# First MLP product: the first two products of seven pairs, instead of three, ahead of half 1 of h^T

## The chip, the core and the metric

One core of a Trainium2 chip runs the whole kernel. The time is device time in microseconds (us) for one execution, inputs and output in HBM; lower is better.

## What is computed

One encoder block on a sequence of 1024 positions with 1024 channels, all in float32. The part that matters here is its second half, the MLP:

```
x  = layer_norm(ALPHA * x + (1 + g1) * mix) * ln1_g + ln1_b      # mix: the mixer's output through w_out
h2 = layer_norm_plain(x) * (1 + sc2) + sh2
ff = square(relu(h2 @ w_ff1 + b_ff1)) @ w_ff2 + b_ff2             # 1024 -> 4096 -> 1024
return layer_norm(ALPHA * x + (1 + g2) * ff) * ln2_g + ln2_b
```

## The kernel before

All matrix products take each operand as the sum of a rounded part and a remainder (type fp32r), and make three matmuls of each product: high x high, high x low, low x high (`mm3`, lines 131 to 133). Rounding is a cast, usually on ScalarE; the remainder is a subtraction, on VectorE or GpSimd.

The first MLP product is h^T = h2 transposed (1024 channels, in 8 blocks `kt` of 128, by 1024 positions) against the 4096 columns of `w_ff1`. It runs as one level of a Strassen-Winograd scheme: positions are cut into two halves of 512, channels into two halves of four blocks, and the columns into 16 pairs (`NPR`) of two blocks of 128. A pair needs seven products instead of eight; each of them is 12 matmuls of 128x128 against 128x512 (4 blocks times three). Its seven right sides are B11 and B21 (half 0 of the positions, plain columns of h^T), B22, T1, T2, T3 and T4 (half 1, or sums and differences with half 1). Its left sides are the plain weight block `w1` (line 945, `w1_plain`), a quarter `w22`, and two blocks `ws` of sums of weights. The first two products of a pair, w1 against B11 and B21, need nothing of half 1.

Around it the order is this. For each half of the positions: the projection by `w_out` (`wo_pass`), the layer norm `ln1` for four tiles of 128 positions (its result `xn2`), and then the transposition into `h_col` (four 128x128 transposes into one PSUM bank of tag c, an ACTIVATE that scales them, line 932). For half 0 the columns are rounded on VectorE (line 967) with the remainder on GpSimd (line 968) and written to HBM (`hb_d`, line 969). For half 1 the T operands are built from them on VectorE: lines 1016, 1017, 1028, 1036 for the sums and `split_h` (936, 937) for rounding. While this goes on TensorE does the first two products of the first three pairs (`EARLY = 3`); their results stay in the six PSUM banks of tags a and b until their pairs come, in the loop over the pairs at the end. Program text: the weights of the early pairs are split ahead of half 1's layer norm, their products stand behind half 1's transposes and T operands.

In that loop, `ff1_products` makes the seven (or remaining five) products of a pair, evicts them with sums (`hidden`), and squares: three of the four results in one VectorE operation (`square`, line 1071), one with a Relu on ScalarE (1106) and a GpSimd multiplication (1107). `ff1_prep` loads the next pair's weights and makes its `ws` on GpSimd (1094 to 1097); `ff1_sums` makes three sums on GpSimd (1140 to 1143) and writes seven tiles of 128x512 to HBM (`hid_d`), from where the second MLP product reads them.

No order between the engines is written by hand in this part. Tiles are declared with a pool, a tag and a number of buffers, and all waits follow from them. The order on each engine and on each DMA queue is fixed when the program is built (`schedule_with_timeline_sim`): instructions are placed by a model of their times, with the program's order as their rank. `xp` holds three raw buffers, of which the gains and offsets of the layer norm (`lg`, `lb`) take two until it is done. Half 0's `xn2` tiles lie in the buffers `wh1` and `wl1`, `w1` in `wh0` and `wl0`. Pool `hp` begins where the layer norm's pools end, and pool `o8p` where those with half 1's `xn2` end.

Of the kernel before, what the change touches and what calls it, by code (L numbers as in the profile page):

```python
# [12 lines left out]
ALU = mybir.AluOpType  # L13
# [13 lines left out]

EARLY = 3

# [59 lines left out]
def body(ctx, tc, x, c, w_ada, b_ada, w_in, b_gate, norm_w, w_out, ln1_g, ln1_b,  # L89
# [20 lines left out]
    def bank(tag):  # L110
        return ps.tile([P, 512], F32, name="ps" + tag, tag=tag, bufs=NB[tag])
# [832 lines left out]

    def w1_plain(i, rv):
        w_ = gw1.tile([P, 2, KT, P], F32R, name="w1", tag=("wh0", "wl0")[i % 2], bufs=1)
# [4 lines left out]
    w1p = {}  # L951
# [22 lines left out]

    KH = KT // 2
    lo, hi = slice(0, KH), slice(KH, KT)
    t2 = [a1w.tile([P, KH, 512], F32R, name=f"t2{n_}", tag=f"w{n_}1", bufs=1) for n_ in "hl"]
# [4 lines left out]

    def s_sums(r0, r1, rs, eng):

        eng.tensor_add(out=rs[:, hi], in0=r1[:, lo], in1=r1[:, hi])
        eng.tensor_sub(out=rs[:, lo], in0=r0[:, lo], in1=r1[:, lo])
        eng.tensor_sub(out=r0[:, lo], in0=rs[:, hi], in1=r0[:, lo])
        eng.tensor_sub(out=r0[:, hi], in0=r0[:, hi], in1=r0[:, lo])
# [10 lines left out]
    def hp_raw(n_):  # L999
        return hp.tile([P, 1024], F32, name=n_, tag="pr", bufs=3)  # L1000

    r0, r1, rs = [hp_raw(n_).rearrange("p (k n) -> p k n", k=KT) for n_ in ("r0", "r1", "rs")]
    tbs = [hp.tile([P, 512], F32, name=f"tb{kt}") for kt in range(KH)]
# [5 lines left out]
    for kt in range(KH):  # L1009
        nc.sync.dma_start(out=hb[kt], in_=hb_d[kt * P:kt * P + P, :])  # L1010
    s_sums(r0, r1, rs, nc.vector)
    for kt in range(KH):
        h_col(hp, kt, xn2s, b12s[kt])
        h_col(hp, KH + kt, xn2s, b22s[kt])
    for kt in range(KH):
        nc.vector.tensor_sub(out=hb[kt], in0=b12s[kt], in1=hb[kt])
        nc.vector.tensor_sub(out=tbs[kt], in0=b22s[kt], in1=hb[kt])
        split_h(tbs[kt], t2[0][:, kt], t2[1][:, kt], nc.vector)
    a1es.close()
    o8es, o8p = pool("o8p", "left")  # L1020
# [23 lines left out]

    hq = lambda kt, lo, x_: hR[:, x_, kt, lo:lo + 512]
    B11 = lambda kt: (hq(kt, 0, 0), hq(kt, 0, 1))
    B21 = lambda kt: (hq(KH + kt, 0, 0), hq(KH + kt, 0, 1))
    B22 = lambda kt: (hq(KH + kt, 512, 0), hq(KH + kt, 512, 1))
# [4 lines left out]

    def prod(pb, a_, b_, first, last):
        for kt in range(KH):
            ks = slice(kt * P, kt * P + P)
            mm3(pb, a_[0][:, ks], a_[1][:, ks], *b_(kt), first and kt == 0, last and kt == KH - 1)

    def quarter(w_, q_):
        return [w_[:, x_].rearrange("p k n -> p (k n)")[:, q_ * 512:q_ * 512 + 512] for x_ in range(2)]  # L1060

    def tq(name, bufs):
        return tp.tile([P, 512], F32, name=name, tag=name, bufs=bufs)

    def hidden(pb, u_, bias):
        h_ = tq("hq", 8)
        nc.vector.scalar_tensor_tensor(out=h_, in0=pb, scalar=bias, in1=u_, op0=ALU.add, op1=ALU.add)
        return h_

    def square(h_):  # L1070
        nc.vector.scalar_tensor_tensor(out=h_, in0=h_, scalar=0.0, in1=h_, op0=ALU.max, op1=ALU.mult)  # L1071
        return h_

    def ff1_first(i):
        pa, pb = bank("a"), bank("b")
        prod(pa, quarter(w1p[i], 0), B11, True, True)
        prod(pb, quarter(w1p[i], 1), B21, True, True)
        return pa, pb

# [7 lines left out]

    def ff1_prep(i):
        r0, r1 = w1_raw(2 * i), w1_raw(2 * i + 1, tp)
        if i not in w1p:  # L1090
            w1p[i] = w1_plain(i, r0)
        w22 = split_22(r1[:, hi])

        nc.gpsimd.tensor_add(out=r1[:, hi], in0=r1[:, lo], in1=r1[:, hi])
        nc.gpsimd.tensor_sub(out=r1[:, lo], in0=r0[:, lo], in1=r1[:, lo])
        nc.gpsimd.tensor_sub(out=r0[:, lo], in0=r1[:, hi], in1=r0[:, lo])
        nc.gpsimd.tensor_sub(out=r0[:, hi], in0=r0[:, hi], in1=r0[:, lo])  # L1097
        return [w22] + split_s((r0, r1), (op8[2 * i % 3], op8[(2 * i + 1) % 3]))

    def ff1_products(i, w22, wa, wb):  # L1100
        ba, bb = bf1[:, 2 * i:2 * i + 1], bf1[:, 2 * i + 1:2 * i + 2]
        pa, pb = early.pop(i) if i in early else ff1_first(i)
        s1 = tq("s1", 2)
        nc.scalar.copy(out=s1, in_=pa)
# [18 lines left out]
        if i:  # L1123
            h21 = square(hidden(pb4, s1, bb))
        pb = bank("a" if i == 0 else "c")
        prod(pb, quarter(wb, 1), T1, True, True)
        h22 = hidden(pb, s1, bb)
# [4 lines left out]
        h12 = square(hidden(pb, u2, ba))  # L1132
        if not i:
            h21 = square(hidden(p4(), s1, bb))
        return h11, h21, h12, h22

    def ff1_sums(i, h11, h21, h12, h22):
# [12 lines left out]
    ops = [split_22(r22)] + ws0  # L1150
    for i in range(NPR):
# [191 lines left out]
```

## Time and profile before

| | |
|---|---|
| three runs | 1126.03, 1127.18, 1129.0 us; median 1127.18 |
| profiled execution | 1127.42 us, its span 1125.4 us |
| mean granted TensorE clock | 0.964 of 2.4 GHz |
| busy share of the span | TensorE 93%, VectorE 74%, ScalarE 36%, GpSimd 33% |
| HBM | 148.29 MB read, 44.05 MB written |

Times in the trace count from the span's start. PE is TensorE, DVE VectorE, ACT ScalarE, POOL GpSimd, SP the queue that issues most DMAs. A granted clock of 1.00 is 2.4 GHz, lower ones are means over stretches at 2.4 and 1.2 GHz. The end of a matmul is modelled, so that a dense stream is read from one start to the next. In the chain, `L131` is line 131, and the line can be that of a helper.

### The profile page before, as it was taken

Reading aid. Unit: us, or ns where it says so; the run is one execution under the profiler, and the core shown is the slowest. Engines: PE = TensorE matmul, PEld = TensorE weight load, DVE = VectorE, ACT = ScalarE, POOL = GpSimd, SP = SyncE. Lnnn points to the kernel's source line nnn. Section 1 sums busy time; section 2 is a strip of 40 time slices with the busy share of each in tenths; the row PEclk is TensorE's granted clock in tenths of the full one; section 3 lists DMA queues with packets and bytes.
Section 4 is the critical chain, followed back from the end, with each engine's and each line's share of the span. In section 5 each row is a group of like instructions: output and inputs, shape, how many; then the busy total and the mean of one; then the engine's idle time right before and its main releaser. Section 6 shows DMA issues by size and latency. Waiting matters only on the chain.

```text
span 1125.4 us, 14177 instructions
## 1 busy us (share of the span) xinstructions
PE 1047.7 (93%) x5033; PEld 854.1 (76%) x5033; DVE 836.1 (74%) x1479; ACT 401.1 (36%) x692; POOL 375.1 (33%) x271
## 2 busy tenths in 40 slices
PE   5899989899999898749999999999998999999995
PEld 3678988797777686538688888888876888888884
DVE  7944775867678499798786766575666797667997
ACT  3353225553455124552222312223243333333420
POOL 3554214634123022209788776765300000000000
PEclk8999989899899899969999999999998999999998
DMA  9916504433133713624545444535987886688502
GB/s 305 289 53 239 184 9 136 132 99 107 58 113 112 253 57 126 210 67 148 187 146 183 147 163 135 174 122 184 342 315 242 285 285 215 206 277 266 169 36 93
DMA packets 140566, 193.27 MB, mean 172 GB/s; under 512 B 9088, under 2 KB 70476, under 8 KB 140496
## 3 DMA queue, kind: packets, MB, share of 16 engines
q1 hardware_dynamic: 121808, 158.81, 42.7%
q10 hardware_dynamic: 18688, 33.56, 8.8%
q8 instruction: 39, 0.64, 0.2%
q14 instruction: 31, 0.25, 0.1%
HBM read 148.29 MB, written 44.05 MB: 171 GB/s over the span
## 4 chain that ended last, share of the span: by engine, by line
PE 45%; DVE 10%; DMA 3%; POOL 2%; issue 2%; ACT 1%; SPq 0%; ACTq 0%; DVEq 0%; POOLq 0%
PE psb L133 6%; PE psb L132 6%; PE psb L131 6%; PE psa L132 5%; PE psa L133 5%; PE psa L131 5%; PE psc L133 4%; PE psc L132 4%; PE psc L131 4%; DMA raw<-in_w_ff_dram 1%; DMA acc<-x_d 1%; DVE ln_st L150 1%; DVE o L1174 1%; DVE acc L1316 1%; DVE acc L914 1%
## 5 line engine op out<-in xcount | busy, mean ns | idle before, releaser
L1173 ACT CAST o<-hraw 128x1024 fp32r<-128x1024 f32 x56 | 58.6, 1050 | 141.9 <-PE psc L133 93.8
L1174 DVE TENSOR_TENSOR o<-hraw,o 128x1024 fp32r<-128x1024 f32 x56 | 71.7, 1284 | 40.9 <-ACT o L1173 40.8
L131 PE MATMUL psa<-wh,hR 128*128 128x256 f32 (+2 forms) x268 | 81.6, 305 | 0.5 <-DVE acc L890 0.5
L133 PE MATMUL psa<-wh,hR 128*128 128x256 f32 (+2 forms) x268 | 80.3, 300 | 0.0
L132 PE MATMUL psa<-wl,hR 128*128 128x256 f32 (+2 forms) x268 | 80.1, 299 | 0.0
L132 PE MATMUL psa<-o,o 128*128 128x512 f32 x176 | 69.4, 394 | 6.9 <-DVE o L1174 6.9
L133 PE MATMUL psa<-o,o 128*128 128x512 f32 x176 | 69.4, 394 | 0.0
L131 PE MATMUL psa<-o,o 128*128 128x512 f32 x176 | 69.0, 394 | 0.2 <-ACT o L1173 0.2
L994 ACT CAST ws<-raw 128x1024 fp32r<-128x1024 f32 x30 | 31.0, 1050 | 104.2 <-POOL raw L1097 94.3
L132 PE MATMUL psb<-o,o 128*128 128x512 f32 x160 | 63.0, 394 | 0.0
L133 PE MATMUL psb<-o,o 128*128 128x512 f32 x160 | 62.9, 393 | 0.0
L261 POOL TENSOR_TENSOR wl<-raw,wh 128x256 fp32r<-128x256 f32 (+2 forms) x27 | 37.9, 1425 | 73.6 <-ACT wh L260 73.6
L131 PE MATMUL psb<-o,o 128*128 128x512 f32 x160 | 62.4, 392 | 0.0
L1140 POOL TENSOR_TENSOR hq<-hq 128x512 f32<-128x512 f32 x16 | 34.5, 2157 | 63.5 <-DVE hq L1071 51.5
L131 PEld LDWEIGHTS psa<-wh,hR 128*128 128x128 f32 x268 | 53.2, 198 | 2.6 <-DVE acc L890 1.2
L132 PEld LDWEIGHTS psa<-wl,hR 128*128 128x128 f32 x268 | 53.1, 198 | 2.0 <-issue 0.9
L133 PEld LDWEIGHTS psa<-wh,hR 128*128 128x128 f32 x268 | 53.0, 198 | 1.1
L995 DVE TENSOR_TENSOR ws<-raw,ws 128x1024 fp32r<-128x1024 f32 x30 | 40.6, 1357 | 13.9 <-ACT ws L994 13.7
L1173 ACT CAST o<-raw 128x1024 fp32r<-128x1024 f32 x32 | 33.3, 1048 | 46.8 <-DVE raw L1216 16.2
L416 POOL TENSOR_TENSOR m<-m,mraw 128x512 f32<-128x512 f32 x28 | 39.7, 1416 | 30.8 <-ACT mraw L415 9.7
L1071 DVE SCALAR_TENSOR_TENSOR hq<-hq 128x512 f32<-128x512 f32 x48 | 49.4, 1031 | 0.6
L132 PEld LDWEIGHTS psa<-o,o 128*128 128x128 f32 x176 | 33.3, 189 | 15.0 <-DVE o L1174 7.7
(434 smaller groups left out, 3154.6 us busy)
## 6 DMA issues: line engine op xcount, KB each, us to landing
raw<-in_w_ff_dram SPq DMA_DIRECT2D x105, 512.0 KB, 4.8
hid_d<-hq SPq DMA_DIRECT2D x112, 256.0 KB, 2.6
hraw<-hid_d ACTq DMA_DIRECT2D x56, 512.0 KB, 4.5
mraw<-in_w_ada_dram SPq DMA_DIRECT2D x32, 512.0 KB, 4.5
raw<-in_w_in_dram SPq DMA_DIRECT2D x10, 512.0 KB, 4.0
xt<-in_x_dram SPq DMA_DIRECT2D x8, 512.0 KB, 5.4
wa<-in_w_ada_dram SPq DMA_DIRECT2D x16, 256.0 KB, 5.8
wa<-in_w_ada_dram SPq DMA_DIRECT2D x8, 512.0 KB, 8.1
```

Of the source, the lines that this page charges most:

```text
L131: nc.tensor.matmul(out=out_ap, lhsT=lh, rhs=rh, start=first, stop=False)
L132: nc.tensor.matmul(out=out_ap, lhsT=lh, rhs=rl, start=False, stop=False)
L133: return nc.tensor.matmul(out=out_ap, lhsT=ll, rhs=rh, start=False, stop=last)
L150: nc.vector.bn_stats(out=st[:, i, :], in_=src[:, i * 512:(i + 1) * 512])
L261: nc.gpsimd.tensor_sub(out=wl, in0=raw, in1=wh)
L416: nc.gpsimd.tensor_add(out=mc, in0=mc, in1=rv[:, i])
L994: nc.scalar.copy(out=w_[:, 0], in_=s_)
L995: nc.vector.tensor_sub(out=w_[:, 1], in0=s_, in1=w_[:, 0])
L1071: nc.vector.scalar_tensor_tensor(out=h_, in0=h_, scalar=0.0, in1=h_, op0=ALU.max, op1=ALU.mult)
L1140: nc.gpsimd.tensor_add(out=sa, in0=h12, in1=h22)
L1173: nc.scalar.copy(out=o_[:, 0], in_=raw)
L1174: eng.tensor_sub(out=o_[:, 1], in0=raw, in1=o_[:, 0])
```

## The change

- `EARLY` is 2, and five more pairs, `SPILL = (3, 5, 7, 9, 11)`, have their first two products made in advance. All seven now stand behind half 1's layer norm and ahead of half 1's transposes in the program. The results of pairs 0 and 1 stay in PSUM. Those of the five are evicted at once into two tiles of a new pool `ep` (one buffer each): the first product as it is (`s1`), the sum of both with bias, Relu and square as `h11`. Both go to HBM by ScalarE's DMA queue and come back in `ff1_prep` of their pair, which also loads the plain weight block again.
- Raw weights of the five are loaded into `wh1` and `wl1`, two to a buffer.
- All squares are Relu and Square on ScalarE.
- Half 0's columns are rounded on ScalarE, their remainders made on VectorE (`split_h`).
- The sums of the first pair's weights are made in place; the buffers `pr` of pool `hp` are two, not three.

```
-EARLY = 3
+SPILL = (3, 5, 7, 9, 11)
+EARLY = 2
...
+    def hidden(h_, pb, u_, bias):
+        nc.vector.scalar_tensor_tensor(out=h_, in0=pb, scalar=bias, in1=u_, op0=ALU.add, op1=ALU.add)
+        return h_
+
+    def square(h_):
+        nc.scalar.activation(out=h_, in_=h_, func=AF.Relu)
+        nc.scalar.activation(out=h_, in_=h_, func=AF.Square)
+        return h_
+
+    def ff1_first(w_):
+        pa, pb = bank("a"), bank("b")
+        prod(pa, quarter(w_, 0), B11, True, True)
+        prod(pb, quarter(w_, 1), B21, True, True)
+        return pa, pb
+
+    def first_sums(i, pa, pb, s1, h11):
+        nc.scalar.copy(out=s1, in_=pa)
+        square(hidden(h11, pb, s1, bf1[:, 2 * i:2 * i + 1]))
+
+    s1_d = dr.tile([len(SPILL) * P, 512], F32, name="s1_d")
+    s1v = lambda i: s1_d[SPILL.index(i) * P:SPILL.index(i) * P + P, :]
     for half in range(2):
         sts = range(half * 4, half * 4 + 4)
         if half:
             for st in sts:
                 wo_pass(0, st)
-            for i in range(EARLY):
-                w1p[i] = w1_plain(i, w1_raw(2 * i))
+            epes, ep = pool("ep", "left")
...
-        if not half:
+        if half:
+
+            for n_, i in enumerate(SPILL):
+                if n_ % 2 == 0:
+                    rw = a1w.tile([P, 2, KT, P], F32, name="rw", tag=("wh1", "wl1")[n_ // 2 % 2], bufs=1)
+                nc.sync.dma_start(out=rw[:, n_ % 2], in_=wf1[:, :, 2 * i * P:2 * i * P + P])
+                pa, pb = ff1_first(w1_plain(rw[:, n_ % 2]))
+                s1, h11 = [ep.tile([P, 512], F32, name=f"e{n}", tag=f"e{n}") for n in ("s1", "h11")]
+                first_sums(i, pa, pb, s1, h11)
+                nc.scalar.dma_start(out=s1v(i), in_=s1)
+                nc.scalar.dma_start(out=hid_d[0, i], in_=h11)
+            early = {i: ff1_first(w1_plain(w1_raw(2 * i))) for i in range(EARLY)}
+        else:
             for kt in range(KT):
                 h32 = h_col(mp, kt, xn2s)
-                nc.vector.tensor_copy(out=hR[:, 0, kt, 0:512], in_=h32)
-                nc.gpsimd.tensor_sub(out=hR[:, 1, kt, 0:512], in0=h32, in1=hR[:, 0, kt, 0:512])
+                split_h(h32, hR[:, 0, kt, 0:512], hR[:, 1, kt, 0:512], nc.vector)
                 nc.sync.dma_start(out=hb_d[kt * P:kt * P + P, :], in_=h32)
...
     def hp_raw(n_):
-        return hp.tile([P, 1024], F32, name=n_, tag="pr", bufs=3)
+        return hp.tile([P, 1024], F32, name=n_, tag="pr", bufs=2)
...
     def ff1_prep(i):
+        if i in SPILL:
+            s1, h11 = tq("s1", 2), tq("hq", 8)
+            nc.sync.dma_start(out=s1, in_=s1v(i))
+            nc.sync.dma_start(out=h11, in_=hid_d[0, i])
+            first = s1, h11
+        else:
+            first = None
         r0, r1 = w1_raw(2 * i), w1_raw(2 * i + 1, tp)
-        if i not in w1p:
-            w1p[i] = w1_plain(i, r0)
+        w1 = w1_plain(r0) if not (i in SPILL or i in early) else None
...
-        h11 = hidden(pb, s1, ba)
-        nc.scalar.activation(out=h11, in_=h11, func=AF.Relu)
-        nc.gpsimd.tensor_mul(out=h11, in0=h11, in1=h11)
+        if first:
+            s1, h11 = first
+        else:
+            pab = early.pop(i) if i in early else ff1_first(w1)
+            s1, h11 = tq("s1", 2), tq("hq", 8)
+            first_sums(i, *pab, s1, h11)
...
         for o_, h_ in enumerate((h11, h21, h12, h22, sa, sb, sc)):
-            nc.sync.dma_start(out=hid_d[o_, i], in_=h_)
-
-    early = {i: ff1_first(i) for i in range(EARLY)}
+            if o_ or i not in SPILL:
+                nc.sync.dma_start(out=hid_d[o_, i], in_=h_)
```

## Rows read from the trace of the kernel before

**Rows 1.** The page, its first part: busy time, share of the span, instructions.

```profile
PE 1047.7 (93%) x5033; PEld 854.1 (76%) x5033; DVE 836.1 (74%) x1479; ACT 401.1 (36%) x692; POOL 375.1 (33%) x271
```

**Rows 2.** The chain that ended last: start, length, what; nothing but PE between these two.

```profile
555.81 0.50 PE psb L133
795.94 0.25 PE psb L133
```

**Rows 3.** Windows: stretch, length, busy us and instructions of each engine, clock, DMA, GB/s.

```profile
440.00:450.00 10.00, 6.67 (x34) 4.65 (x33) 10.00 (x16) 3.75 (x9) 5.20 (x3) 1.00 0.49 189
...
480.00:490.00 10.00, 1.22 (x2) 0.50 (x2) 10.00 (x17) 9.09 (x16) 0.00 (x0) 0.56 0.11 42
490.00:500.00 10.00, 6.16 (x17) 4.35 (x18) 10.00 (x17) 1.84 (x3) 0.00 (x0) 0.58 0.24 79
...
579.10:598.20 19.10, 19.10 (x84) 15.37 (x83) 11.25 (x14) 4.69 (x6) 15.05 (x12) 1.00 0.51 176
```

**Rows 4.** Timeline of PE, 455 to 511: start, length, line, what it writes and reads.

```profile
455.25 0.38 PE L929 MATMUL psc<-cs,wl 128*128 128x128 f32 x2
...
471.53 0.39 PE L133 MATMUL psb<-hR,w 128*128 128x512 f32 x1
471.76 0.38 PE L929 MATMUL psc<-cs,xn2q 128*128 128x128 f32 x2
...
510.64 0.40 PE L131 MATMUL psa<-t4h,w 128*128 128x512 f32 x1
```

**Rows 5.** Windows of 5 us with gaps on PE, columns as in rows 3.

```profile
535.00:540.00 5.00, 4.17 (x18) 3.10 (x18) 5.00 (x4) 1.80 (x3) 4.30 (x3) 1.00 0.42 120
...
550.00:555.00 5.00, 3.91 (x17) 2.79 (x16) 2.26 (x3) 2.95 (x3) 1.55 (x2) 1.00 0.03 11
```

**Rows 6.** Groups by line, 440 to 820: busy us, mean ns, idle before.

```profile
L1071 DVE SCALAR_TENSOR_TENSOR hq<-hq 128x512 f32<-128x512 f32 x48 | 49.4, 1031 | 0.6
...
L1107 POOL TENSOR_TENSOR hq<-hq 128x512 f32<-128x512 f32 x16 | 17.7, 1108 | 43.0 <-ACT hq L1106 43.0
...
L1067 DVE SCALAR_TENSOR_TENSOR hq<-psb,cols,s 128x512 f32<-128x512 f32 x16 | 11.9, 747 | 16.9 <-issue 14.0 <-POOL hq L1141 2.9
...
L1106 ACT ACTIVATE hq<-hq 128x512 f32<-128x512 f32 x16 | 10.1, 630 | 7.1 <-DVE hq L1067 7.1
...
L936 ACT CAST t2h<-tb 128x512 fp32r<-128x512 f32 x4 | 2.5, 618 | 2.3 <-DVE tb L1017 2.3
```

**Rows 7.** Groups by line, ACT over the whole span.

```profile
L118 ACT ACT_TABLE_LOAD x1 | 1.3, 1283 | 0.7 <-PEq L1329 0.7
```

**Rows 8.** DMA issues, 380 to 560: queue, count, KB each, median us to landing.

```profile
raw<-in_w_ff_dram SPq DMA_DIRECT2D x15, 512.0 KB, 4.8
hid_d<-hq SPq DMA_DIRECT2D x18, 256.0 KB, 3.8
```

**Rows 9.** Groups by line, 435 to 470.

```profile
L968 POOL TENSOR_TENSOR hR<-h,hR 128x512 fp32r<-128x512 f32 x8 | 10.3, 1285 | 10.0 <-DVE hR L967 6.2 <-DVE rs_u L140 1.7 <-DVE rs_u L141 1.5
...
L967 DVE CAST hR<-h 128x512 fp32r<-128x512 f32 x8 | 6.8, 847 | 0.0
...
L948 DVE TENSOR_TENSOR w<-raw,w 128x1024 fp32r<-128x1024 f32 x1 | 1.2, 1207 | 0.0
```

**Rows 10.** Timelines of ACT and of DVE, 439 to 479, columns as in rows 4.

```profile
439.83 1.42 ACT L932 ACTIVATE h<-psc,sc 128x512 f32<-128x512 f32 x2
...
449.06 0.29 ACT L138 ACTIVATE rs_u<-ln_ve 128x1 f32<-128x1 f32 x2 [3.98 <-DVE ln_ve L153]
...
468.97 1.23 ACT L159 ACTIVATE xn2k<-acc,ln_nm,rs_r 128x1024 f32<-128x1024 f32 x1
...
455.87 2.35 DVE L909 SCALAR_TENSOR_TENSOR acc<-acc,ln_mv,lg 128x1024 f32<-128x1024 f32 x1
...
458.35 0.41 DVE L967 CAST hR<-h 128x512 fp32r<-128x512 f32 x1
...
478.13 0.69 DVE L937 TENSOR_TENSOR hR<-b,hR 128x512 fp32r<-128x512 f32 x1
```

More of the change, by code (lines that the diff above doesn't have):

```diff
@@ L943, in w1_raw, with w1_plain @@
         return rv
-    def w1_plain(i, rv):
-        w_ = gw1.tile([P, 2, KT, P], F32R, name="w1", tag=("wh0", "wl0")[i % 2], bufs=1)
+    n_w1 = [0]
+    def w1_plain(rv):
+        n_w1[0] += 1
+        w_ = gw1.tile([P, 2, KT, P], F32R, name="w1", tag=("wh0", "wl0")[n_w1[0] % 2], bufs=1)
         nc.scalar.copy(out=w_[:, 0], in_=rv)
@@ L949, in w1_plain, with quarter, prod @@
         return w_
-    w1p = {}
+    def quarter(w_, q_):
+        return [w_[:, x_].rearrange("p k n -> p (k n)")[:, q_ * 512:q_ * 512 + 512] for x_ in range(2)]
+    hq = lambda kt, lo, x_: hR[:, x_, kt, lo:lo + 512]
+    KH = KT // 2
+    lo, hi = slice(0, KH), slice(KH, KT)
+    B11 = lambda kt: (hq(kt, 0, 0), hq(kt, 0, 1))
+    B21 = lambda kt: (hq(KH + kt, 0, 0), hq(KH + kt, 0, 1))
+    def prod(pb, a_, b_, first, last):
+        for kt in range(KH):
+            ks = slice(kt * P, kt * P + P)
+            mm3(pb, a_[0][:, ks], a_[1][:, ks], *b_(kt), first and kt == 0, last and kt == KH - 1)
+    def hidden(h_, pb, u_, bias):
[15 more added lines that the diff above has]
+    s1v = lambda i: s1_d[SPILL.index(i) * P:SPILL.index(i) * P + P, :]
     for half in range(2):
@@ L981, in body, with s_sums @@
     hs = slice(512, 1024)
[L983 to L987, printed above, removed]
+    def s_sums(r0, r1, eng):
+        eng.tensor_add(out=r1[:, hi], in0=r1[:, lo], in1=r1[:, hi])
+        eng.tensor_sub(out=r1[:, lo], in0=r0[:, lo], in1=r1[:, lo])
+        eng.tensor_sub(out=r0[:, lo], in0=r1[:, hi], in1=r0[:, lo])
         eng.tensor_sub(out=r0[:, hi], in0=r0[:, hi], in1=r0[:, lo])
@@ L999, in hp_raw @@
     def hp_raw(n_):
-        return hp.tile([P, 1024], F32, name=n_, tag="pr", bufs=3)
-    r0, r1, rs = [hp_raw(n_).rearrange("p (k n) -> p k n", k=KT) for n_ in ("r0", "r1", "rs")]
+        return hp.tile([P, 1024], F32, name=n_, tag="pr", bufs=2)
+    r0, r1 = [hp_raw(n_).rearrange("p (k n) -> p k n", k=KT) for n_ in ("r0", "r1")]
     tbs = [hp.tile([P, 512], F32, name=f"tb{kt}") for kt in range(KH)]
@@ L1010, in body @@
         nc.sync.dma_start(out=hb[kt], in_=hb_d[kt * P:kt * P + P, :])
-    s_sums(r0, r1, rs, nc.vector)
+    s_sums(r0, r1, nc.vector)
     for kt in range(KH):
@@ L1018, in body @@
         split_h(tbs[kt], t2[0][:, kt], t2[1][:, kt], nc.vector)
+    epes.close()
     a1es.close()
@@ L1052, in body @@
     T4 = lambda kt: t34[KH + kt]
[L1054 to L1060, printed above, removed]
     def tq(name, bufs):
         return tp.tile([P, 512], F32, name=name, tag=name, bufs=bufs)
[L1065 to L1078, printed above, removed]
     def split_22(src):
@@ L1088, in ff1_prep, with ff1_products @@
     def ff1_prep(i):
+        if i in SPILL:
[5 more added lines that the diff above has]
+            first = None
         r0, r1 = w1_raw(2 * i), w1_raw(2 * i + 1, tp)
-        if i not in w1p:
-            w1p[i] = w1_plain(i, r0)
+        w1 = w1_plain(r0) if not (i in SPILL or i in early) else None
         w22 = split_22(r1[:, hi])
[L1094 to L1100, printed above, removed]
-        ba, bb = bf1[:, 2 * i:2 * i + 1], bf1[:, 2 * i + 1:2 * i + 2]
-        pa, pb = early.pop(i) if i in early else ff1_first(i)
-        s1 = tq("s1", 2)
-        nc.scalar.copy(out=s1, in_=pa)
-        h11 = hidden(pb, s1, ba)
-        nc.scalar.activation(out=h11, in_=h11, func=AF.Relu)
-        nc.gpsimd.tensor_mul(out=h11, in0=h11, in1=h11)
+        s_sums(r0, r1, nc.gpsimd)
+        return [first, w1, w22] + split_s((r0, r1), (op8[2 * i % 3], op8[(2 * i + 1) % 3]))
+    def ff1_products(i, first, w1, w22, wa, wb):
+        ba, bb = bf1[:, 2 * i:2 * i + 1], bf1[:, 2 * i + 1:2 * i + 2]
+        if first:
[4 more added lines that the diff above has]
+            first_sums(i, *pab, s1, h11)
         def p4():
@@ L1123, in ff1_products @@
         if i:
-            h21 = square(hidden(pb4, s1, bb))
+            h21 = square(hidden(tq("hq", 8), pb4, s1, bb))
         pb = bank("a" if i == 0 else "c")
         prod(pb, quarter(wb, 1), T1, True, True)
-        h22 = hidden(pb, s1, bb)
+        h22 = hidden(tq("hq", 8), pb, s1, bb)
         nc.vector.tensor_tensor(out=u2, in0=pb, in1=u2, op=ALU.add)
@@ L1131, in ff1_products @@
         prod(pb, quarter(wa, 1), B22, True, True)
-        h12 = square(hidden(pb, u2, ba))
+        h12 = square(hidden(tq("hq", 8), pb, u2, ba))
         if not i:
-            h21 = square(hidden(p4(), s1, bb))
+            h21 = square(hidden(tq("hq", 8), p4(), s1, bb))
         return h11, h21, h12, h22
```

9 lines of the change are left out of this document (2 added, 7 removed).

## Prediction

> **What bounds the kernel now.** I read the page first: TensorE is busy 93% of a span of 1125.4 us [rows 1]; the profiled execution took 1127.42 us, 2.0 us outside its span, and the median of the three runs is 1127.18, so the profile stands for them (0.2 us apart). A measurement of this kernel can tell about 0.3%, 3.4 us, from no change. Then I read the chain that ended last. Up to about 503 us it is made of short VectorE pieces, then it hops between GpSimd, VectorE and issue, and from 555.81 to 795.94 nothing but matmuls is in it [rows 2]. So the edit touches two stages with different limits: the half-1 layer norm with the building of h^T (VectorE sets the end), and the first MLP product (TensorE sets it).
>
> The table of windows shows the first of these: from 440 to 450 VectorE is full and TensorE two thirds busy; from 480 to 490 VectorE is full and TensorE has 1.22 us of work, at a granted clock of 0.56; in a window of 19.1 us further on TensorE is full at clock 1.00 [rows 3]. That last window gives the price of a matmul: 19.10/84 = 0.2274 us, so one pair's first two products (24 matmuls) are 5.46 us and one product of 12 is 2.73.
>
> The TensorE timeline then shows where the early work stands. The last transpose of half 0 comes at 455.25; half 1's transposes start in earnest at 471.76, right behind the last early matmul at 471.53; pair 0's last product is over when the next one starts at 510.64 [rows 4]. I use that 510.64 as the mark: all that precedes it is the head, all behind it is the product stage.
>
> **The change, part by part.** *The gain.* Seven pairs instead of three have their first two products ahead: 4 x 5.46 = 21.8 us of matmuls leave the product stage. That stage's chain is matmuls from 555.8 to 795.9 [rows 2], so it shortens by all of it, if the operands keep up. Pairs 0 to 2 are short in the kernel before (five products, 13.7 us) and there TensorE is idle 0.83 us in 535-540 and 1.09 in 550-555, where the chain goes through GpSimd [rows 5]. Now two short pairs stand in a row, not three, the other five alternate with full ones, and GpSimd loses its square (1.1 us a pair [rows 6]). Of the 1.9 us I take 1.0 back (bounds 0 and 1.9).
>
> *Squares on ScalarE.* Per pair three VectorE squares of 1.031 us and one GpSimd square of 1.108 go; ScalarE gets seven more operations like the Relu, 0.630 us [rows 6]. The trace has no Square; its price lies between 0.63 (a Relu of that shape) and 0.63 with a table load of 1.28 [rows 7] before every change of function. Relu already runs between other functions, and the whole trace has one load [rows 7], so I take 0.63. ScalarE's load in the stage is 4.69 us per full pair [rows 3]; with 7 x 0.63 it is 9.1 of 19.1. TensorE hides it: cost nothing. Without that cover each square would be 0.23 us later (1.26 against 1.03); with loads everywhere ScalarE would pass 19 us per pair and cost some 10 to 15 us in all.
>
> *The way by HBM.* Each spilled pair loads its 512 KB weight block twice, writes two 256 KB tiles and reads them back, and writes one tile less at its end. DMA is about half busy in the stage [rows 3], so this is hidden there (bounds 0 and the 4.8 us of a load for one late read). In the head, the one tile for h11 cycles through the sum with bias 0.75, two ScalarE operations 1.26 and a write of 3.8 us [rows 6, 8]: 5.8 us a pair against 5.46 of matmuls, 1.7 us over five pairs. Three banks per tag absorb that; I take 0 (bounds 0 and 1.7).
>
> *Half 0's rounding.* Eight VectorE casts (847 ns) become eight ScalarE casts (0.62 us); eight GpSimd subtractions (1285 ns) become VectorE ones (0.69, as L937 at 478.13) [rows 6, 9, 10]. The GpSimd ones also stretch VectorE: a cast takes 0.41 us at 458.35 and 0.85 in the mean, and the 1024-wide L909 takes 2.35 us at 455.87, where L948 of that width takes 1.2 [rows 9, 10]. That is 8 x 0.44 = 3.5 us in the casts and 1.1 in L909, 4.6 in all. VectorE gains 6.8 - 5.5 = 1.3 on the operations, 1.1 on L909, and 2.4 because two weight splits that stood in this layer norm now come behind it: about 5 us. Half 1's last normalised tile, ready at 470.2 [rows 10], would be there near 465. The page "SBUF — State Buffer" of the Trainium skill, section "Who interferes with whom", says that a VectorE instruction with two SBUF inputs and a GpSimd instruction that reads SBUF exclude each other for a whole instruction. By that rule up to the full 8 x 1.285 = 10.3 us would come back instead of 4.6, and the tile would be there near 459, nearer to rival B; the measured stretch agrees in kind and is less than half of that.
>
> *What moves ahead of half 1's h^T.* In the text of the program the seven pairs now stand before half 1's transposes; the three stood behind them. The trace shows TensorE doing its list in order: the transposes at 471.76 come behind the early matmuls, though the last of their inputs was there at 470.2 [rows 4, 10]. So the question is when the seven start and whether the transposes get between them. Start: per column block ScalarE now does 0.71 (two in 1.42) and 0.62, so eight from 439.83 [rows 6, 10] take until 450.5, and the last transpose stands near 449.5. Only then do the two buffers come free that the new raw loads use (half 0's normalised tiles lie there). A load takes 4.8 us [rows 8], the split 1.2 on VectorE [rows 9] and as much at most on ScalarE: first products at about 457. Seven pairs: 38.2 us; for a slow start I add 1.5, between 0 and 3.2: from 490 to 500, at clock 0.58 behind an idle stretch, 17 matmuls took 6.16 us [rows 3], 0.36 each, and 24 of them would be 3.2 over 5.46. They end at 496.7. The split of pair k + 2 (2.4 us) fits inside pair k + 1, so no gap opens in which a transpose, later in the text, would be taken first.
>
> *What is late next.* Half 1's transposes then start at 496.7 instead of 471.8, and VectorE's chain over the T operands behind them, at about 498. Before, it ran from 478.13 to the mark at 510.64, 32.5 us [rows 4, 10]; of it two of the sums of weights (1.2) and two weight splits (2.4) are done by now, since VectorE is free while the seven run: 28.9 us. New mark: 526.9, which is 16.3 us later.
>
> **Sum.** 1127.4 - 21.8 + 16.3 - 1.0 = 1120.9: 1121 us. Most of what the stage gives is paid in the head, because TensorE is idle again under VectorE's T chain.
>
> **Rivals.**
> *A, the forecast, 0.50.* Seven pairs first, T chain behind. With a start between 453 and 462: 1117 to 1126.
> *B, transposes in between, 0.20.* If half 1's tiles are ready before the first weights are split, or the order written down leaves gaps, the T chain runs beside the products. Then TensorE bounds the head: 457 + 38.2 + 13.7 + about 7 of transposes = 516, 5.3 us late: 1127.4 - 21.8 + 5.3 - 1.0 = 1110. For it speaks that VectorE has room for both once the layer norm is done; against it the program order.
> *C, the stage doesn't give it back, 0.12.* Spilled pairs have 13.7 us of matmuls against 15.05 - 1.1 = 14 us of GpSimd [rows 3, 6]. If each of the five waits as pairs 1 and 2 do now (0.8 to 1.1 us [rows 5]), 4 to 6 us are lost: 1125 to 1127. Against it: each stands beside a full pair with 5 us to spare.
> *D, half 0's columns don't come sooner, slower, 0.18.* ScalarE's list is in order and mixes the columns with layer-norm steps that wait for VectorE, once for 3.98 us [rows 10]. If the copies only add to it, the last transpose moves from 455.25 to 460.2, not to 449.5, the first products start at 467.4 by the same steps, and everything behind is 10.4 us later: 1131. It decides from a start at 463.5 on, where the gain is used up. Two chances in a hundred of this are the table loads.
>
> **Numbers.** Faster by over 0.3% (below 1123.8): 0.41 of A, all of B, 0.01 of C: 0.62. Within 0.3%: 0.08 of A, 0.10 of C, 0.03 of D: 0.21. Slower: the rest, 0.17. The range takes in B and D: 1107 to 1132; A's own is 1115 to 1127.
>
> **What would show it.** Right, if the timeline has the first spilled product near 457, seven pairs without a break, half 1's transposes behind them near 497, VectorE nearly idle between the end of the layer norm and there, and pair 0's last product near 527; and the matmuls of the stage running without gaps for 21.8 us less. Transposes among the products would show B; gaps before the spilled pairs 3, 5, 7, 9 and 11 would show C; a first spilled product behind 463 shows D. What would make it wrong is above all the order in which TensorE's list was written, which I infer and the trace of before doesn't show.

## The result, and the profile after

The changed kernel takes 1115.57 us (median of four runs, 1113.65 to 1116.65); the kernel before, run beside it, 1126.76 (four runs, 1126.03 to 1129.0). The ratio is 0.9895, 95% interval 0.9875 to 0.9916: faster by 1.05%, 11.2 us, where 6 were forecast. The direction held and the time lies inside the range; the size was missed by 5.3 us.

The profiled execution took 1116.65 us, its span is 1114.8. In the page's first part, which answers to [rows 1], VectorE has lost 60 us of work and GpSimd 53, ScalarE has gained 68:

```profile
PE 1044.6 (94%) x5033; PEld 856.5 (77%) x5033; DVE 776.6 (70%) x1431; ACT 469.4 (42%) x812; POOL 322.2 (29%) x247
```

The timeline of PE, columns as in [rows 4], gives the places that the prediction named: the last transpose of half 0, the first spilled product, the last product of the seven with half 1's transposes right behind it, and pair 0's last product, of which the first and the twelfth matmul and the next start are shown.

```profile
447.88 0.64 PE L931 MATMUL psc<-cs,wl 128*128 128x128 f32 x2
...
453.92 0.80 PE L133 MATMUL psa<-hR,w 128*128 128x512 f32 x1 [2.38 <-ACT w L952]
...
498.63 0.39 PE L135 MATMUL psb<-hR,w 128*128 128x512 f32 x1
498.87 0.27 PE L931 MATMUL psc<-cs,xn2k 128*128 128x128 f32 x1
...
520.50 0.50 PE L133 MATMUL psa<-t4h,w 128*128 128x512 f32 x1 [0.59 <-ACT w L1104]
...
523.52 0.39 PE L135 MATMUL psa<-t4h,w 128*128 128x512 f32 x1
523.75 0.40 PE L133 MATMUL psa<-t4h,w 128*128 128x512 f32 x1
...
788.05 0.39 PE L133 MATMUL psa<-o,o 128*128 128x512 f32 x1
```

The last of these lines has its counterpart in the kernel before:

```profile
796.01 0.39 PE L131 MATMUL psa<-o,o 128*128 128x512 f32 x1
```

So the mark moved from 510.64 [rows 4] to 523.75, 13.1 us later. The product stage, from the mark to the first matmul of the second MLP product (`psa<-o,o`, at 796.01 before and 788.05 now), went from 285.4 to 264.3, 21.1 us shorter. What follows it went from 329.4 to 326.8. These are the whole difference of the spans: 13.1 - 21.1 - 2.6 = -10.6.

The windows of the head, columns as in [rows 3]:

```profile
450.00:460.00 10.00, 6.13 (x13) 4.03 (x14) 10.00 (x28) 4.70 (x10) 0.00 (x0) 0.50 1.07 312
...
480.00:490.00 10.00, 10.00 (x47) 8.05 (x46) 7.88 (x13) 7.05 (x12) 0.00 (x0) 1.00 0.33 113
490.00:500.00 10.00, 9.57 (x46) 7.50 (x44) 4.38 (x6) 4.71 (x8) 0.00 (x0) 1.00 0.38 125
500.00:510.00 10.00, 5.76 (x21) 4.27 (x22) 10.00 (x15) 10.00 (x17) 0.00 (x0) 0.72 0.00 0
```

TensorE is now nearly full from 480 to 500 (10.00 and 9.57 us), where it had 1.22 and 6.16 us of work before [rows 3], and VectorE has room there. Behind 500 the picture turns: VectorE and ScalarE are full with the T chain and TensorE is 5.76 us busy at a granted clock of 0.72. That is the head of forecast A. The twelve matmuls of pair 0's last product begin with one more wait, 0.59 us at 520.50, for a cast of their weights on ScalarE.

The timeline of VectorE shows how much of the T chain was left by then: of its 36 operations on half 1's columns and the T operands (lines 939, 1063, 1064, 1076 and 1084) nine stand before the end of the seven pairs, from 480.41 on, and the other 27 begin at 499.99. In the same view VectorE stood still for 7.09 us before the sum of the second spilled pair; the next weight split came late by it and TensorE waited 0.51 us before 476.51:

```profile
474.57 0.75 DVE L971 SCALAR_TENSOR_TENSOR eh<-psb,cols,es 128x512 f32<-128x512 f32 x1 [7.09 <-DMA hid_d<-eh]
...
480.41 0.69 DVE L1063 TENSOR_TENSOR hb<-b,hb 128x512 f32<-128x512 f32 x1
...
499.99 0.69 DVE L1064 TENSOR_TENSOR tb<-b,hb 128x512 f32<-128x512 f32 x1 [3.15 <-ACT b L934]
```

For the comparisons below one place ahead of every edit is needed, because executions differ there. I take VectorE's first gain step of the layer norm: 410.69 in the profiled execution of before, 410.68 after. "Head" is the time from it to the mark (before 99.95, after 113.07), "start" the time from it to the first early product, "stage" as above, "rest" what follows.

```profile
410.69 1.27 DVE L909 SCALAR_TENSOR_TENSOR acc<-acc,ln_mv,lg 128x1024 f32<-128x1024 f32 x1
```

```profile
410.68 1.27 DVE L911 SCALAR_TENSOR_TENSOR acc<-acc,ln_mv,lg 128x1024 f32<-128x1024 f32 x1
```

### The profile page after: what moved, and what is told of

The parts are those of the page before. It is cut to its first block, busy times and chain, and to the rows that moved or that the text cites. A ratio compares the mean times of both kernels' runs of the same rounds, so it can differ in the third digit from the quotient of the medians.

```text
span 1114.8 us, 14281 instructions
## 1 busy us (share of the span) xinstructions
PE 1044.6 (94%) x5033; PEld 856.5 (77%) x5033; DVE 776.6 (70%) x1431; ACT 469.4 (42%) x812; POOL 322.2 (29%) x247
## 4 chain that ended last, share of the span: by engine, by line
PE 53%; DVE 4%; DMA 2%; issue 1%; POOL 1%; ACT 0%; DVEq 0%; SPq 0%; POOLq 0%; ACTq 0%
PE psb L135 7%; PE psb L134 7%; PE psb L133 7%; PE psa L135 6%; PE psa L134 6%; PE psa L133 6%; PE psc L134 5%; PE psc L135 5%; PE psc L133 5%; DMA raw<-in_w_ff_dram 1%; DMA rw<-in_w_ff_dram 1%; DMA hid_d<-eh 0%; DVE acc L1340 0%; DVE hR L939 0%; DVE acc L1297 0%
## 5 line engine op out<-in xcount | busy, mean ns | idle before, releaser
L975 ACT ACTIVATE hq<-hq 128x512 f32<-128x512 f32 x59 | 37.1, 630 | 58.3 <-DVE hq L971 58.3
L1032 POOL TENSOR_TENSOR raw<-raw 128x512 f32<-128x512 f32 x15 | 20.3, 1355 | 95.9 <-DVE w L1105 93.2
L1164 POOL TENSOR_TENSOR hq<-hq 128x512 f32<-128x512 f32 x16 | 22.9, 1429 | 80.6 <-ACT hq L976 64.6
L134 PEld LDWEIGHTS psa<-o,o 128*128 128x128 f32 x176 | 33.3, 189 | 13.7 <-DVE o L1198 6.4
```

The lines of the kernel that those rows point to most:

```text
L134: nc.tensor.matmul(out=out_ap, lhsT=lh, rhs=rl, start=False, stop=False)
L975: nc.scalar.activation(out=h_, in_=h_, func=AF.Relu)
L1032: eng.tensor_add(out=r1[:, hi], in0=r1[:, lo], in1=r1[:, hi])
L1164: nc.gpsimd.tensor_add(out=sa, in0=h12, in1=h22)
```

## The experiments

Twelve kernels, in three groups with the kernel before beside each (medians 1126.1, 1126.51 and 1126.18). Times are medians, ratios stand to the kernel before with 95% intervals; the other columns are of each kernel's profiled execution. All in us.

| kernel | early pairs | time | ratio | start | head | stage | rest |
|---|---|---|---|---|---|---|---|
| before | 3 | 1126.76 | 1 | 32.3 | 99.9 | 285.4 | 329.4 |
| changed | 2 + 5 | 1115.57 | 0.9895 [0.9875, 0.9916] | 43.2 | 113.1 | 264.3 | 326.8 |
| rounding alone | 3 | 1120.55 | 0.9941 [0.9924, 0.9959] | 31.3 | 95.1 | 284.9 | 328.5 |
| squares alone | 3 | 1123.4 | 0.998 [0.9968, 0.9991] | 32.2 | 99.4 | 283.0 | 329.1 |
| side edits only | 3 | 1118.61 | 0.9922 [0.9898, 0.9947] | 31.2 | 95.8 | 282.4 | 327.2 |
| one spilled | 2 + 1 | 1116.8 | 0.9917 [0.9904, 0.993] | 44.5 | 94.6 | 282.0 | 327.5 |
| three spilled | 2 + 3 | 1117.53 | 0.9925 [0.9912, 0.9938] | 43.1 | 102.2 | 275.5 | 326.9 |
| squares back | 2 + 5 | 1121.68 | 0.9955 [0.9937, 0.9972] | 43.2 | 111.5 | 270.2 | 328.9 |
| rounding back | 2 + 5 | 1117.33 | 0.9914 [0.9896, 0.9931] | 46.4 | 114.2 | 264.2 | 327.1 |
| two PSUM pairs last | 2 + 5 | 1113.17 | 0.9881 [0.9869, 0.9894] | 43.0 | 108.5 | 262.6 | 328.5 |
| raws through `xp` | 2 + 5 | 1106.92 | 0.982 [0.9793, 0.9847] | 31.3 | 104.1 | 260.9 | 328.2 |
| pairs behind transposes | 2 + 5 | 1105.26 | 0.9797 [0.9774, 0.9819] | 31.3 | 105.0 | 260.9 | 327.9 |
| one behind transposes | 2 + 1 | 1116.77 | 0.9924 [0.9904, 0.9944] | 31.2 | 95.4 | 282.2 | 327.4 |
| six behind transposes | 2 + 6 | 1103.39 | 0.9793 [0.9779, 0.9807] | 31.5 | 107.7 | 255.3 | 327.7 |

The differences of the last three columns add up to the difference of the times within 2.5 us in every row.

**Fewer spilled pairs.** The line `SPILL` alone is changed, to one pair and to three.

```
-SPILL = (3, 5, 7, 9, 11)
+SPILL = (3,)          # the other kernel: (3, 7, 11)
```

> One spilled pair (3) instead of five, so three pairs ahead as in the kernel before, all else as changed. Theory 1 (what a pair saves in the stage it costs again in the head once TensorE is full there): the three are done near 472, when half 1's last tile is ready, pair 0's last product comes near 502 instead of 524, the stage is 21.8 us longer, and the time is within 3 us of the changed kernel's 1115.6. Rival (the gain is the pairs' own, in proportion to their number): four pairs fewer cost most of the 11 us, 1123 to 1127.

> Three spilled pairs (3, 7, 11), five ahead. Theory 1: the five are done near 485, pair 0's last product comes near 513, the stage is 10.9 us longer, time 1113 to 1117. Rival (gain in proportion): 1119 to 1122.

From one spilled pair to five the stage shrinks by 17.7 and the head grows by 18.5; the times are 1116.8, 1117.5 and 1115.6, the middle one half a us above its range, and their intervals overlap. In this order four more pairs ahead are paid for in the head in full. With one spilled pair, and so as many early pairs as before, the kernel already has nearly the whole gain, so most of it must come from elsewhere.

**Side edits only.** No spilled pair; three early pairs at their old places in the program, their weights split ahead of half 1's layer norm as before; squares, rounding and the sums in place as changed.

```
-SPILL = (3, 5, 7, 9, 11)
-EARLY = 2
+SPILL = ()
+EARLY = 3
...
+            ew = [w1_plain(w1_raw(2 * i)) for i in range(EARLY)]
...
+    early = {i: ff1_first(ew[i]) for i in range(EARLY)}
     hpes.close()
```

> The kernel before with the side edits alone: three pairs in PSUM, split ahead of half 1's layer norm and their products behind half 1's transposes, nothing spilled, but squares on ScalarE and half 0's rounding on ScalarE with its remainders on VectorE, and the weight sums in place. Theory 1: the layer norm of half 1 is done some 5 us sooner and so is pair 0's last product, near 505; the stage as before less 1: 1119 to 1122. Rival (the side edits do nothing by themselves, the seven pairs make the whole gain): 1125 to 1128.

The time is 7.5 us below the kernel before and just below the range of theory 1: two thirds of the change's gain without a single pair more. Its six runs spread over 10 us (1110.5 to 1120.8) and its profiled execution is the quickest of them; that execution is 7.4 us ahead already at the place where "head" begins, which is why the columns count from there.

**Each side edit by itself, in the kernel before.** Rounding alone takes `split_h` for half 0's columns; squares alone makes all squares Relu and Square on ScalarE.

```
-                nc.vector.tensor_copy(out=hR[:, 0, kt, 0:512], in_=h32)
-                nc.gpsimd.tensor_sub(out=hR[:, 1, kt, 0:512], in0=h32, in1=hR[:, 0, kt, 0:512])
+                split_h(h32, hR[:, 0, kt, 0:512], hR[:, 1, kt, 0:512], nc.vector)
```

> The kernel before with one edit: half 0's rounding on ScalarE and its remainders on VectorE. Theory after the run with the side edits alone (GpSimd's subtractions held VectorE for nearly their whole length, so half 1's layer norm ends some 12 us sooner): half 1's last tile ready near 458 instead of 470, pair 0's last product near 499 instead of 510.6, time 1115 to 1120. Rival (my 5 us by the stretched rows): last tile near 465, pair 0's last product near 506, 1121 to 1124. A third (the squares or the weight sums in place made it): no change, 1125 to 1128.

```
-        nc.vector.scalar_tensor_tensor(out=h_, in0=h_, scalar=0.0, in1=h_, op0=ALU.max, op1=ALU.mult)
+        nc.scalar.activation(out=h_, in_=h_, func=AF.Relu)
+        nc.scalar.activation(out=h_, in_=h_, func=AF.Square)
...
-        nc.scalar.activation(out=h11, in_=h11, func=AF.Relu)
-        nc.gpsimd.tensor_mul(out=h11, in0=h11, in1=h11)
+        square(h11)
```

> The kernel before with one edit: all squares are Relu and Square on ScalarE. Theory (the squares matter only where several short pairs stand in a row, and the kernel before has three of those): the head stays as it was, mark within 1 us of 510.6; the stage behind it is 1 to 3 us shorter than 285.4; time 1123 to 1126. Rival (VectorE and GpSimd hold the stage everywhere, also at full pairs): the stage is 6 us shorter or more, time 1120 or less. Second rival (the squares touch nothing here): stage within 0.5 us, time 1126 to 1127.

Rounding alone brings 6 us, nearly all of it in the head (-4.9): with three early pairs the chain behind half 1's last normalised tile sets the mark. The timeline of ScalarE has that tile's last step (`xn2k`, at 468.97 before [rows 10]) here:

```profile
464.96 1.23 ACT L159 ACTIVATE xn2k<-acc,ln_nm,rs_r 128x1024 f32<-128x1024 f32 x1
```

It is ready at 466.2 and not at 470.2, and the mark stands at 506.2: what the rival of the 5 us said, not the theory of 12. Squares alone bring 2 to 3 us, 2.4 of them in the stage, as expected. The two together (6.0 and 2.8) give about what the side edits give (7.5); the sums in place and the two buffers of `pr` were not run by themselves.

**Each side edit undone, in the changed kernel.** Squares back on VectorE and GpSimd, then half 0's rounding back on VectorE with its remainder on GpSimd; the lines are those of the last two diffs, turned round.

> The changed kernel with the squares as before: three a pair in one VectorE operation, h11's by Relu on ScalarE and a multiplication on GpSimd (for the spilled pairs too). Theory (TensorE bounds the stage, so who squares costs nothing): within 2 us of the changed kernel's 1115.6. Rival (VectorE and GpSimd, relieved, are what lets the spilled pairs run without gaps; or the 2.6 us found behind the stage come from there): 1118 to 1122, with gaps on TensorE at the short pairs.

> The changed kernel with half 0's rounding as before: casts on VectorE, remainders on GpSimd. Theory (the seven pairs start when half 0's last transpose frees the raw buffers, and everything is queued behind them): last transpose of half 0 near 455 instead of 448, first early product 5 to 7 us later than 454, pair 0's last product as much later than 524, time 1120 to 1123. Rival (the seven pairs are bounded by their splits and writes, not by their start): within 2 us of 1115.6.

Without the rounding the kernel loses 1.8 us, inside the rival's 2 and with overlapping intervals; in the kernel before the same edit was worth 6. Here the seven pairs and the T chain behind them set the mark; they start 3.2 us later, not 5 to 7, and the head is 1.1 us longer. Without the squares it loses 6.1, and my theory of "within 2" fell. The head is even 1.6 us shorter; the stage is 5.9 us longer. One window of the stage shows it, first in the changed kernel, then with the squares back:

```profile
600.00:640.00 40.00, 40.00 (x174) 32.17 (x173) 19.11 (x24) 16.46 (x25) 27.46 (x21) 1.00 0.62 204
```

```profile
600.00:640.00 40.00, 37.71 (x155) 29.74 (x154) 27.69 (x31) 7.41 (x9) 30.14 (x20) 0.96 0.56 181
```

The two longest entries of the latter's table of waits from 520 to 790 (in all, times, longest):

```profile
PE psc L133 <- DVE u L1153: 2.0, 1, 2.0
PE psb L133 <- ACT ws L1042: 1.8, 1, 1.8
```

The first of GpSimd's three sums of results, from the groups by line of 520 to 780, in the changed kernel and with the squares back:

```profile
L1164 POOL TENSOR_TENSOR hq<-hq 128x512 f32<-128x512 f32 x15 | 21.1, 1408 | 64.6 <-ACT hq L976 64.6
```

```profile
L1165 POOL TENSOR_TENSOR hq<-hq 128x512 f32<-128x512 f32 x15 | 29.9, 1995 | 42.8 <-DVE hq L975 33.8 <-issue 9.0
```

The same 40 us hold 19 matmuls fewer, 4.4 us at 0.233 a matmul (worked out in the next section): TensorE is idle for 2.29 of them, of which the wait of 1.8 is the larger part (the one of 2.0 lies just ahead of the window), and its clock is 0.96 in the mean. What stood in front of the two waits is on the timelines, with the squares back. The wait of 2.0 is for the sum at 598.12, and VectorE does one of its squares, 1.03 us, right before it. The wait of 1.8 is for `ws`, which ScalarE can round only when GpSimd's weight sums, begun at 626.40, are done:

```profile
597.16 1.03 DVE L975 SCALAR_TENSOR_TENSOR hq<-hq 128x512 f32<-128x512 f32 x1
598.12 0.68 DVE L1153 TENSOR_TENSOR u<-psc,u 128x512 f32<-128x512 f32 x1
```

```profile
632.64 1.99 ACT L1042 CAST ws<-raw 128x1024 fp32r<-128x1024 f32 x2 [7.66 <-POOL raw L1036]
```

```profile
626.40 1.29 POOL L1033 TENSOR_TENSOR raw<-raw 128x512 f32<-128x512 f32 x1 [3.08 <-DVE w L1106]
```

GpSimd's sum takes 1.995 us with the squares on VectorE and 1.408 without; over its eight groups of 128x512 sums it is 187.8 us against 167.8 for the same 15 pairs, and its own squares, 1.19 us each, come on top. That is 13.7 us a pair against 11.2, where the five products of a short pair take 14.0 (60 matmuls at 0.233). In neither kernel is VectorE or GpSimd full over the window; one wait came through VectorE and one through GpSimd. Whether VectorE's squares or GpSimd's alone would have been enough to keep the loss away was not tried.

**Where the seven pairs stand.** First, only the two pairs that stay in PSUM are moved, behind the T operands:

```
-            early = {i: ff1_first(w1_plain(w1_raw(2 * i))) for i in range(EARLY)}
...
+    early = {i: ff1_first(w1_plain(w1_raw(2 * i))) for i in range(EARLY)}
     hpes.close()
```

> Only the place in the program of the two pairs that stay in PSUM is changed: behind half 1's transposes and T operands, as their three stood before; the five spilled pairs stay ahead. In TensorE's list three blocks of eight transposes now stand among the last matmuls of the seven pairs, where the changed kernel has them behind all seven. Theory 1 (the head is held by TensorE's order: the T chain on VectorE can't start before the seven are done): the T operands start some 10 us sooner and run beside the last two pairs, pair 0's last product moves from 524 to about 517, where TensorE's own work bounds it (454 + 3 of slow start + 38.2 + 7 of transposes + 13.7 = 516), and the time is 1108 to 1110. Rival (the head is held by something else, the weight splits or VectorE): pair 0's last product stays within 2 us of 524 and the time at 1114 to 1117.

24 instead of 15 of the 32 transposes of half 1 now come before the last early product, the head is 4.6 us shorter, the time 2.4: the mark nearly as theory 1 expected (518.2), the time, 1113.2, in neither range, and its interval overlaps that of the changed kernel. Then all seven are moved behind half 1's transposes, and the raw weights of the five come through the three buffers of `xp`:

```
-                if n_ % 2 == 0:
-                    rw = a1w.tile([P, 2, KT, P], F32, name="rw", tag=("wh1", "wl1")[n_ // 2 % 2], bufs=1)
-                nc.sync.dma_start(out=rw[:, n_ % 2], in_=wf1[:, :, 2 * i * P:2 * i * P + P])
-                pa, pb = ff1_first(w1_plain(rw[:, n_ % 2]))
...
         h_col(hp, KH + kt, xn2s, b22s[kt])
+    for i in SPILL:
+        pa, pb = ff1_first(w1_plain(w1_raw(2 * i)))
```

> All seven pairs behind half 1's transposes in the program, the two PSUM pairs behind the T operands too; the raw weights of the five then come through the three buffers of pool xp, since half 1's T2 takes the buffers they had. Theory (order on TensorE holds the T chain): in TensorE's list the transposes stand in blocks among the products, from the second pair on. Pair 0's last product comes near 516, where TensorE's own work bounds it, stage as in the changed kernel: 1107 to 1110. Rival (the raw weights come too slowly with one free buffer until the layer norm's gains are released, or the T chain competes with the splits on VectorE): pair 0's last product at 522 or later, 1114 or more.

10.3 us faster than the changed kernel, the mark at 515.4, the time a little below the theory's range. But this edit did two things, and its trace shows the first product 12 us sooner. So I separated them: the changed kernel with nothing but the other buffers.

```
-                if n_ % 2 == 0:
-                    rw = a1w.tile(...)
-                nc.sync.dma_start(out=rw[:, n_ % 2], in_=wf1[:, :, 2 * i * P:2 * i * P + P])
-                pa, pb = ff1_first(w1_plain(rw[:, n_ % 2]))
+                pa, pb = ff1_first(w1_plain(w1_raw(2 * i)))
```

> The changed kernel with one edit: the raw weights of the five spilled pairs are loaded through the three raw buffers of the other weights, not into the buffers of half 0's normalised tiles. The order in the program stays, the pairs ahead of half 1's transposes. Theory 'start' (what made the kernel with the pairs behind the transposes 10 us faster is mostly that its first product begins at 441.8 and not at 453.9): first product at 440 to 444, mark 512 to 516, time 1104 to 1108. Theory 'order' (it is that transposes and products mix): first product sooner, but the mark stays at 521 or later, time 1112 to 1116.

8.7 us faster than the changed kernel with the order of the program untouched: theory "start" held. On TensorE, too, the order is nearly that of the changed kernel: 16 of half 1's 32 transposes stand before the last early product, there 15. The timelines of SP show the first raw load for an early pair, in the changed kernel and in this one:

```profile
448.12 0.38 SPq L1007 DMA_DIRECT2D rw<-in_w_ff_dram  x1
```

```profile
416.31 0.38 SPq L944 DMA_DIRECT2D raw<-in_w_ff_dram  x1
```

This kernel's first early product on PE's timeline, and one of its windows:

```profile
436.35 0.71 PE L133 MATMUL psa<-hR,w 128*128 128x512 f32 x2
```

```profile
450.00:460.00 10.00, 8.79 (x38) 6.62 (x37) 8.62 (x23) 6.07 (x9) 0.00 (x0) 1.00 0.75 227
```

The load no longer waits for half 0's last transpose (447.88 in the changed kernel), so products go in between while half 0's columns are made: in the window of 450 to 460 TensorE is 8.79 us busy at clock 1.00, where the changed kernel has 6.13 at 0.50 (9.19 at 1.00 in 444.4 to 454.4, the same stretch counted from where "head" begins). The profiled execution here is the quickest of five (1099.97 to 1109.72) and 5.6 us ahead where "head" begins, so that on the changed kernel's count its first product stands at 441.9 and its mark at 514.7, both as theory "start" had them. The head is 9.0 us shorter than in the changed kernel, the stage 3.4 shorter and the rest 1.4 longer.

**How many pairs, once they start early.** The kernel with the pairs behind the transposes, with `SPILL = (3,)` and with `SPILL = (3, 5, 7, 9, 11, 13)`.

> As the kernel with the early pairs behind half 1's transposes (1105.3 us), but one spilled pair, not five: three early pairs in all. Theory (behind the transposes the T chain runs beside the products, so four more pairs cost the head less than the 21.8 us that they save in the stage): the stage is about 20 us longer (281), the mark only 8 to 12 us sooner (503 to 507), time 1113 to 1118. Rival (the number of pairs does not matter here either, only the order and the sooner start): the mark is about 20 us sooner (495), time 1104 to 1107.

> As the kernel with the early pairs behind half 1's transposes (1105.3 us), with six spilled pairs (3, 5, 7, 9, 11, 13). Theory (with eight early pairs TensorE holds the head, so a further one saves 5.5 us in the stage and costs 5 to 5.5 in the head): time 1104 to 1106. Rival (there is still room under the T chain): 1100 to 1102.

From three to seven early pairs the head grows by 9.6 and the stage shrinks by 21.3, so here the pairs pay: 11.5 us by the times. The eighth adds 2.7 to the head and takes 5.6 from the stage; the time falls by 1.9, between the two ranges expected, and the intervals of the two overlap. 1103.39 us, ratio 0.9793, is the best of all kernels run. With three early pairs neither the place nor the sooner start makes a difference (1116.8 in front of the transposes with a start of 44.5, 1116.77 behind them with 31.2).

## Why the prediction was right in direction and wrong in size

The gain came out nearly twice as large as forecast. On the profiled executions three terms of the sum were off: the head, 16.3 us forecast and 13.1 measured; the stage, -22.8 and -21.1; and what follows the stage, for which the sum had nothing and the traces show -2.6. The step that failed in the largest of them is the one that put the whole T chain behind the seven pairs because no gap would open for a transpose; the step that gave the gain to the wrong edit is "cost nothing" for the squares.

**The head, mechanism right in the main, term 3.2 us too large.** The prediction had seven pairs first and the T chain behind them, the mark 16.3 later; it came 13.1 later. The start was seen for the right reason (the buffers of half 0's normalised tiles): 453.9 against 457. The seven took longer than the 39.7 us expected, 45.0. 3.5 us of that were lost on the first 18 matmuls, from 453.92 to 461.65, with a wait for weights of 0.90 us in between: in 450 to 460 TensorE did 13 matmuls at clock 0.50, and a raw load took 7.8 us to landing, not the 4.8 of [rows 8]. The rest are transposes in between, one wait of 0.51 us and a price of a matmul that was read too low (below). They ended at 498.9, 2.2 us later than forecast; that it is only 2.2 is luck, since the sooner start and the longer work nearly cancel. The step that failed is "no gap opens in which a transpose, later in the text, would be taken first": 15 of 32 transposes came before the last early product, which is the sign that the prediction had named for B, nine T operations were done by then, and from 499.99 the chain needed 23.8 us to the mark, not 28.9.

**The stage, 1.7 us too large.** Forecast -21.8 - 1.0, measured -21.1. The 1.0 for gaps did not come: TensorE waited 1.98 and 0.83 us for the weights of the next T4 product, where it had lost 1.9 in such gaps before [rows 5], and the matmuls behind the waits came at 0.43 us each up to 541.80.

```profile
537.09 0.50 PE L133 MATMUL psa<-t4h,w 128*128 128x512 f32 x1 [1.98 <-ACT w L1104]
...
538.65 0.79 PE L135 MATMUL psa<-t4h,w 128*128 128x512 f32 x1 [0.83 <-DVE w L1105]
```

The price of a matmul in the sum, 0.2274, is a little too low as well: the window's 84 count matmuls that lie only partly in it. From one start to the next, twelve in the kernel before took 2.80 us, 0.233 each, as these two starts of products on PE's timeline show:

```profile
583.87 0.39 PE L131 MATMUL psb<-hR,w 128*128 128x512 f32 x1
...
586.67 0.39 PE L131 MATMUL psc<-t2h,ws 128*128 128x512 f32 x1
```

By that price the four pairs are 22.4 us and not 21.8, and the seven 39.2 and not 38.2.

**What follows the stage** went down by 2.6, a term that the sum did not have. 1.7 of it can be found. In the second MLP product of the kernel before TensorE waits 29.2 us behind its start for operands that VectorE splits:

```profile
825.22 0.50 PE L132 MATMUL psa<-o,o 128*128 128x512 f32 x1 [0.95 <-DVE o L1174]
```

Only the three kernels with the old squares have this wait (before, rounding alone, squares back); it is gone with squares alone, and none of the other kernels has it. With it the next long wait ends 52.51 us into that product, in the changed kernel 50.81. So this, too, came with the squares. In the other kernels the rest lies between 326.9 and 329.1, with squares alone at 329.1 although the wait is gone, so that what else moves it, the other 0.9 included, stays open. With 0.2 outside the span these make the 4.3 us by which the profiled execution undercuts the forecast (-3.2 + 1.7 - 2.6 - 0.2); the median is another 1.1 lower.

**Squares, "cost nothing", the step that misread the change.** This step did not make the time wrong, since the sum was made for a kernel with the squares on ScalarE; it made the account of the gain wrong. That TensorE hides them on ScalarE was right, and so was the price, as ScalarE's groups by line from 440 to 820 show for Relu and Square:

```profile
L976 ACT ACTIVATE hq<-hq 128x512 f32<-128x512 f32 x59 | 37.2, 632 | 2.0 <-DVE ws L1042 0.6
L975 ACT ACTIVATE hq<-hq 128x512 f32<-128x512 f32 x59 | 37.1, 630 | 58.3 <-DVE hq L971 58.3
```

But the -21.8 of the pairs was worked out as if the stage would give it with the squares anywhere. It does not: with the squares back it gives 15.2. Their worth is 6 us here and 2 to 3 in the kernel before, and the reading that fits both is that four more pairs have five products of matmuls instead of seven to hide VectorE and GpSimd under. Rival C named that loss with the right size (4 to 6 us) and had 14 us of GpSimd a pair; what it missed is that the squares on ScalarE kept the loss away, by GpSimd's sums (20.0 us less over 15 pairs) as much as by the one square that the prediction took off.

**Rounding: right in size, unused in the sum.** Half 1's last tile was expected 5 us sooner; by itself the edit makes it 4.0 sooner, counted from the same place 4.4, and the kernel 6 us faster. By the rule of the Trainium skill's page "SBUF — State Buffer", section "Who interferes with whom", the prediction had worked out that up to 10.3 us of stretch would come back and the tile would be ready near 459; the measured tile is far from that, so the rows decide. In the changed kernel the tile is not early at all (471.7). ScalarE's timeline there shows its step behind an eviction of a spilled product that waited for TensorE:

```profile
468.82 0.59 ACT L986 COPY es<-psa 128x512 f32<-128x512 f32 x1 [2.31 <-PE psb L135]
...
470.45 1.24 ACT L161 ACTIVATE xn2k<-acc,ln_nm,rs_r 128x1024 f32<-128x1024 f32 x1
```

**What the pairs are worth.** The forecast gave them nearly all of the gain and the side edits almost none. The runs say the opposite: side edits -7.5, four more pairs in this place -1 to -3 (one spilled pair 1116.8, side edits only 1118.6, changed 1115.6; the intervals overlap, so that the pairs' share is not clear of the noise). B's transposes came in part, but its head and D's did not; B's time of 1110 is passed as soon as the first load does not wait.

## What to carry to other kernels

Work moved ahead of a bound stage pays only as far as it fits under a wait that is already there; read where its first load may start, because a buffer that is free late can cost more than the order of the instructions. Cost an edit in the kernel that the other edits make, not in the one before: the rounding was worth 6 us alone and 2 in company, the squares 2 to 3 alone and 6 in company. And when a stage is shortened by taking matmuls out of it, take its other engines' work per matmul as a new bound, even where none of them is full.

## What was not expected of the hardware

Profiled executions differ by up to 7.4 us before any of the edits begin. In 200 to 300 us, which no edit touches, the changed kernel's profiled execution has a granted clock of 0.91 and 579 matmuls, that of the side edits alone 0.97 and 612:

```profile
200.00:300.00 100.00, 94.62 (x579) 79.64 (x578) 79.14 (x253) 50.11 (x141) 37.56 (x32) 0.91 0.34 103
```

```profile
200.00:300.00 100.00, 96.60 (x612) 80.45 (x611) 79.27 (x260) 52.48 (x147) 37.43 (x33) 0.97 0.36 111
```

What decides between them was not tried. The second surprise is how long single transfers take while the DMA share is full: the five raw loads of 512 KB in 440 to 480 took 7.8 us in the median (share 1.07 and 1.12 in two windows of ten; 4.8 in [rows 8]), and VectorE's 7.09 us stop above came from a write of 256 KB that ScalarE's queue issued at 468.90, behind a copy that waited for TensorE, and that held the one buffer of `h11` until 474.5.

```profile
rw<-in_w_ff_dram SPq DMA_DIRECT2D x5, 512.0 KB, 7.8
```

The third is GpSimd's sums: the same instructions take 12% longer in the kernel in which VectorE does squares of two SBUF operands (187.8 against 167.8 us). The page "SBUF — State Buffer" of the Trainium skill, section "Who interferes with whom", states that a VectorE instruction with two SBUF inputs contends with a GpSimd instruction that reads SBUF; the trace agrees in kind.
